# A hybrid transformer layer on one core: one weight tile loaded earlier, four pieces of work moved, and a second pool for the score banks

## The chip, the cores and the metric

The kernel runs on one core of a Trainium2 chip. The metric is the device time of one execution in microseconds. A comparison uses the median of several executions of each kernel on the same chip. A profile is one more execution, recorded by the hardware profiler; its span and its own time are given beside the medians.

## The reference

One layer (`DEPTH` is 1) of a backbone over 1024 latent tokens and 256 context tokens, `D_MODEL` 1024, all in float32:

```python
mod_x = (silu(c) @ w_ada + b_ada)           # six vectors: shift, scale, gate, twice
px = modulate(rms_norm(x, norm1_w), sh1, sc1) @ w_in     # latent tokens
pc = modulate(rms_norm(ctx, norm1_w), csh1, csc1) @ w_in # context tokens
# columns of w_in: q, k, v, z, a, b of a gated DeltaNet (4 heads of 128),
#                  q, k, v of a neighbourhood attention (8 heads of 64)
x = x + g1 * (concat([dn_x, na_x]) @ w_out)
x = x + g2 * swiglu(modulate(rms_norm(x, norm2_w), sh2, sc2), w_ffn_in, w_ffn_out)
```

The DeltaNet group passes q, k and v through a depthwise convolution of five taps and SiLU, normalises q and k, and runs a chunked scan in both directions, context first. For each chunk a unit triangular matrix has to be inverted. The attention group uses one softmax over a 16-wide window of eight rows and all context keys. Only the latent stream is returned.

## The kernel before, in words

Every large product is made with float32 operands that are split into a high part of type float32r (`hi`, `hh`, `whi`) and a rest (`lo`, `hl`, `wlo`), and takes three matmuls: high times high, high times rest, rest times high. The 1280 tokens lie along the free dimension in three segments of 256, 512 and 512 columns (`SEGS`), the model dimension in eight tiles of 128 partitions (`KT`).

*The start* (lines 665 to 778). SP loads the eight token tiles `xt` (640 KB each, line 680), two weight tiles `raws` (line 684) and the eight tiles `wada` of the first modulation weights (1024 KB each, `load_ada`, line 674). ACT squares the token tiles, DVE adds them in pairs (line 740), TensorE sums over partitions with a matrix of ones (line 742, two passes for each segment), and ACT turns the sums into the norm's factors `rs` (logarithm, line 744; exponential, line 745). `ada(j)` (line 701) multiplies one `wada` tile by the two conditioning vectors, 16 matmuls, and copies the row out; `column(j)` (line 710) turns that row into per-partition columns, four matmuls and two small DVE operations. `normed_tile(k)` (line 721) then makes `hh[k]` and `hl[k]` of token tile `k`: DVE multiplies (726), ACT adds the shift and rounds (727), DVE takes the rest (729). The first two key heads (`first`) are multiplied with each tile as it comes (lines 754 to 775). In this part the order of TensorE, DVE and ACT is written out by hand (`manual_schedule`): each of these engines runs its instructions in the order of the program text.

*The rest of the first half* (lines 1067 to 1157). The list `jobs` holds blocks of the input projection: key heads 0 to 3, one half of the gate z with the columns a and b (`Wide("z", 1)`), attention keys, values, queries and so on, in the end the other half of z (`Wide("z", 0)`). Each `Block` job has eight k steps (`mm([k])`); its `evac` copies the result to a tile `cacc`, of which there are two, and for q, k and v applies the five taps on DVE. As long as only the first PSUM pool exists (jobs 0 to 4), all banks come from one ring of eight, and DVE reads the taps straight from the block's three banks (line 455). `silu`, `norm` and the generator `finish` (line 530) follow one and two jobs later: for a key head `finish` makes three groups of transposes (line 537), three groups of products of the keys with themselves (line 561), and then a mask and stores. In a Block job one step of `finish` is taken after each k step from k = 3 on (line 1136), in a Wide job after each tile of tokens (line 1114), and what is left at the end of the job.

Outside the part written by hand, a planner puts the instructions on the engines: the order of the program text is their rank, and by its cost model it lets a later instruction go first where an earlier one is not ready; `keep_in_program_order` excepts single instructions from that. An engine then runs its list strictly in order, and waits where the model was wrong.

Two background lists are stepped along with the k steps. `bg` holds the block inverses and `preps` (line 948), which prepares the chunks for the scan: first products at L1000 from factors `rg` that POOL makes (line 988), an exponential, DVE's multiplication of `kk` (1011), products L1024, and three further levels (1035). Its first preparation is held back by `LATE` steps. `bg2` holds `modulation` (line 208), which makes the remaining modulation vectors: DVE accumulates weight rows (line 238), and `reduce` sums the result over partitions on TensorE (line 223), four steps after the last row where there is one accumulator.

[...] From job 5 on a pool `psa` gives four banks to blocks, two to `m`, two to `pr`. Ahead of the last job, `Wide("z", 0)`, it is closed and a pool `psg` opened, which holds two plain banks (`ps`) and two score tiles of three banks each (`sc`) of the attention; attention (`pair`, line 292) and scan then share TensorE until 790 us. The output projection and the feed-forward part follow with their own pool.

## Time and profile before

| | us |
|---|---|
| median of three runs | 1515.09 (1510.95 to 1518.55) |
| the profiled execution's own time | 1512.36 |
| its span | 1510.6 |
| TensorE busy | 1462.2 |
| VectorE (DVE) busy | 996.8 |
| ScalarE (ACT) busy | 703.5 |
| GpSimd (POOL) busy | 236.7 |

All times within the profile count from the start of its span. PE is TensorE, PEld its weight loads, SP the queue that issues most transfers. A line such as `PE m L223 <- DVE acc L238: 2.0, 1, 2.0` says that TensorE's instruction of line 223, which writes a tile `m`, waited for DVE's of line 238, 2.0 us in all, once, 2.0 us at most. A row of the time line gives start, duration, engine, line, operation, what it writes and reads, and in brackets how long the engine had been idle and who released it. A row of the stretches gives the stretch, its length, the busy time (with the count of instructions), the granted clock as a share of full speed, the share of the DMA engines that was busy, and GB/s.

### The profile page before, as it was taken

The page shows a single profiled execution, that of the slowest core. Times are in us where ns is not written, and L with a number is a line of the kernel's source. Part 1 is how long each engine was busy: PE and PEld are TensorE (multiplying, and loading weights), DVE is VectorE, ACT ScalarE, POOL GpSimd, SP SyncE. Part 2 cuts the span into 40 slices and gives each one's busy share as a digit, 9 for nine tenths or more (in the row PEclk, how much of TensorE's full clock was granted, in tenths as well). Part 3 has the DMA queues.
Part 4 walks back from the last instruction along what each step waited for, and adds up shares of the span by engine and source line. Part 5 has one row for each costly group of instructions (what it writes and reads, how often), then busy time and mean ns, then how long its engine had stood idle before and what let it go on. Part 6 is the DMA issues. An engine that isn't in the chain of part 4 may idle for free.

```text
span 1510.6 us, 23890 instructions
## 1 busy us (share of the span) xinstructions
PE 1462.2 (97%) x8702; PEld 1223.5 (81%) x8702; DVE 996.8 (66%) x1716; ACT 703.5 (47%) x1389; POOL 236.7 (16%) x286
## 2 busy tenths in 40 slices
PE   6999999999999998999999999999999999999998
PEld 3788797877788877887878888888888888888887
DVE  5773589875463745778867389766665567598652
ACT  5453442456663246656853284333333334354440
POOL 1054601456652201111210000000000000000000
PEclk9999999999999999999999999999999999999999
DMA  9274122778665569998539205433333335798742
GB/s 389 75 215 143 54 78 72 244 222 248 195 191 174 157 187 291 290 263 279 163 112 343 79 28 166 141 105 105 105 105 105 105 105 174 260 360 279 251 140 84
DMA packets 205398, 267.36 MB, mean 177 GB/s; under 512 B 15968, under 2 KB 113760, under 8 KB 204256
## 3 DMA queue, kind: packets, MB, share of 16 engines
q1 hardware_dynamic: 197680, 260.01, 53.2%
q10 hardware_dynamic: 7600, 5.81, 1.2%
q8 instruction: 69, 1.13, 0.3%
q14 instruction: 49, 0.40, 0.1%
HBM read 201.02 MB, written 68.94 MB: 179 GB/s over the span
## 4 chain that ended last, share of the span: by engine, by line
PE 51%; ACT 1%; DVE 1%; issue 0%; DMA 0%; POOL 0%; DVEq 0%; POOLq 0%; ACTq 0%
PE ps L1398 28%; PE ps L1741 14%; PE ps L1527 3%; PE ps L1375 1%; PE ps L1549 1%; PE sc L332 1%; PE sc L322 1%; PE sc L309 1%; PE ps L1252 0%; PE ps L1261 0%; DMA z<-z_d 0%; ACT sq L1302 0%; ACT bt L315 0%; DVE bt L313 0%; PE ps L223 0%
## 5 line engine op out<-in xcount | busy, mean ns | idle before, releaser
L1459 ACT CAST uhi<-wq 128x512 fp32r<-128x512 f32 x101 | 61.3, 622 | 135.9 <-issue 84.6
L413 PE MATMUL blk<-hh,whi 128*128 128x512 f32 (+1 forms) x410 | 121.0, 389 | 1.6 <-ACT kk L562 1.4
L1459 ACT CAST uhi<-ws 128x512 fp32r<-128x512 f32 x91 | 54.0, 621 | 146.3 <-PE ps L1398 91.4
L413 PE MATMUL blk<-hl,whi 128*128 128x512 f32 (+1 forms) x410 | 113.4, 370 | 0.3 <-DVE hl L729 0.3
L609 PE MATMUL blk<-zw,hh 128*128 128x256 f32 (+1 forms) x576 | 112.3, 289 | 1.0 <-ACT cr L461 1.0
L413 PE MATMUL blk<-hh,wlo 128*128 128x512 f32 (+1 forms) x410 | 112.0, 370 | 0.6 <-POOL wlo L204 0.6
L1460 DVE TENSOR_TENSOR ulo<-wq,uhi 128x512 fp32r<-128x512 f32 x101 | 67.6, 688 | 59.1 <-ACT uhi L1459 32.7
L1398 PE MATMUL ps<-hT,uhi 128*128 128x512 f32 x336 | 103.7, 390 | 0.0
L1398 PE MATMUL ps<-lT,uhi 128*128 128x512 f32 x336 | 103.4, 389 | 0.0
L1398 PE MATMUL ps<-hT,ulo 128*128 128x512 f32 x336 | 103.4, 389 | 0.0
L609 PEld LDWEIGHTS blk<-zw,hh 128*128 128x128 f32 x576 | 90.7, 189 | 4.1 <-ACT cr L461 1.4
L1398 PE MATMUL ps<-hB,uhi 128*128 128x512 f32 x288 | 89.1, 390 | 0.0
L1398 PE MATMUL ps<-lB,uhi 128*128 128x512 f32 x288 | 88.7, 389 | 0.0
L1398 PE MATMUL ps<-hB,ulo 128*128 128x512 f32 x288 | 88.7, 389 | 0.0
L413 PEld LDWEIGHTS blk<-hh,wlo 128*128 128x128 f32 x410 | 71.0, 188 | 14.8 <-POOL wlo L204 0.9
L413 PEld LDWEIGHTS blk<-hl,whi 128*128 128x128 f32 x410 | 71.2, 188 | 14.4 <-DVE hl L729 0.8
L609 PE MATMUL blk<-zw,hl 128*128 128x256 f32 (+1 forms) x288 | 81.9, 284 | 0.0
L413 PEld LDWEIGHTS blk<-hh,whi 128*128 128x128 f32 x410 | 67.6, 190 | 16.8 <-issue 3.8
L204 POOL TENSOR_TENSOR wlo<-wraw,whi 128x1024 fp32r<-128x1024 f32 x18 | 44.8, 2488 | 186.8 <-ACT whi L203 186.5
L1398 PEld LDWEIGHTS ps<-lT,uhi 128*128 128x128 f32 x336 | 63.1, 188 | 13.1
L1398 PEld LDWEIGHTS ps<-hT,ulo 128*128 128x128 f32 x336 | 63.1, 188 | 13.1
L1398 PEld LDWEIGHTS ps<-hT,uhi 128*128 128x128 f32 x336 | 62.9, 188 | 13.0
(361 smaller groups left out, 3500.7 us busy)
## 6 DMA issues: line engine op xcount, KB each, us to landing
wq<-w_fo SPq DMA_DIRECT2D x99, 256.0 KB, 4.2
wq<-w_gu SPq DMA_DIRECT2D x88, 256.0 KB, 2.9
wad<-wa SPq DMA_DIRECT2D x64, 256.0 KB, 4.3
bt<-rpb SPq DMA_DIRECT2D x64, 192.0 KB, 3.9
t_d<-g SPq DMA_DIRECT2D x22, 512.0 KB, 3.5
fr<-t_d SPq DMA_DIRECT2D x44, 256.0 KB, 4.9
f_d<-g SPq DMA_DIRECT2D x33, 256.0 KB, 2.1
fr<-f_d SPq DMA_DIRECT2D x33, 256.0 KB, 4.2
```

Source lines behind the costliest of these rows:

```text
L204: lo_engine.tensor_tensor(o, r, h.bitcast(F32), OP.subtract)
L309: s = pe.matmul(sc[:, u * 640 + n0:u * 640 + n1], q, ks[i], start=i == 0, stop=i == 1)
L322: pe.transpose(sc[:, u * 640 + j * 128:u * 640 + (j + 1) * 128], bt[:, j * 128:(j + 1) * 128], ident)
L332: pe.matmul(sc[u * ND:u * ND + ND, 1280:1408], vv, pt[:, j * 128:(j + 1) * 128], start=j == 0, stop=j == 4)
L413: pe.matmul(o, ww[:, k], xx[k][:, s], start=k == 0 and j == 0, stop=k == KT - 1 and j == 2)
L609: pe.matmul(p[:, :c1 - c0], x[k][:, s], ww[:, k, c0:c1], start=k == 0 and j == 0, stop=k == KT - 1 and j == 2)
L1375: pe.matmul(o, w[wi][:, k], parts[xi][k][:, s], start=k == 4 and j == 0, stop=k == 3 and j == 2)
L1398: pe.matmul(o, w[wi][:, k], x[xi][:, k], start=first and k == 0 and j == 0, stop=k == n - 1 and j == 2, skip_group_check=True)
L1459: act.copy(hi, self.raw[key])
L1460: dve.tensor_tensor(lo, self.raw[key], hi.bitcast(F32), OP.subtract)
L1527: pe.matmul(o, w[wi][:, k], parts[xi][k][:, s], start=k == 0 and j == 0, stop=k == KT - 1 and j == 2)
L1741: pe.matmul(o[b], w[wi][:, b], F[xn, p][xi], start=n in (0, 1, 5) and p == 0 and j == 0, stop=p == NFB // 2 - 1 and j == 2, skip_group_che ...
```

## The change

- `load_ada(0)` is issued between token tiles 3 and 4, and `ada(0)` and `column(0)` stand ahead of the third pair of squares.
- `normed_tile` is cut into `high` and `low`; the logarithm and exponential of each segment follow each other, and the first tile's `high` of a segment comes one segment later. The split of the first weights (`prefetch`) stands ahead of the logarithms. `ada(1)` stands behind the first six products, `column(1)` behind the second six.
- In job 3, `finish` of key head 1 starts at k = 5, not 3, and what is left at its end goes to the next job, one step after each tile, ahead of key head 2's.
- `reduce` of `modulation` with one accumulator comes six steps after the last row, not four.
- `LATE` is 6, not 7, and the first preparation has three steps, not two, between L1000 and L1024.
- Ahead of the last job a pool `psc` with the score tiles is opened first, and one score tile is taken at once; `psg` keeps the plain banks.

```diff
@@ -241,7 +241,7 @@
                     reduce(q - 1, prev)
             prev = acc2
             if sums == 1:
-                for _ in range(4):
+                for _ in range(6):
                     yield
                 reduce(q, prev)
                 prev = None
@@ -292,7 +292,7 @@
         def pair(heads, bts, vw, vc, half, cb, out):
             r0 = 4 * half
-            sc = psum[-1].tile([128, 1536], F32, name="sc", tag="sc", bufs=2)
+            sc = psc.pop() if len(psc) > 1 else psc[0].tile([128, 1536], F32, name="sc", tag="sc", bufs=2)
             mx = nw.tile([128, 2, 4], F32, name="mx", tag="mx", bufs=3)
             for u, (head, w0, bt) in enumerate(zip(heads, WIN, bts)):
                 qs, kh, kl = head
@@ -368,7 +368,7 @@
         next(old)
         store(*done)
-    na, kept = [], []
+    na, kept, psc = [], [], []
     def store(out, hp, half):
@@ -676,13 +676,15 @@
                 sp.dma_start(w, a["wa1"][j])
             for k in range(KT):
+                if k == 4:
+                    load_ada(0)
                 x = xp.tile([128, T], F32, name=f"xt{k}", tag=f"xt{k}")
                 sp.dma_start(x, a["xcT"][k])
                 xt.append(x)
             raws = [xp.tile([128, KT, 128], F32, name=f"fraw{i}", tag=f"fraw{i}") for i in range(2)]
             for i in range(2):
                 sp.dma_start(raws[i], a["w_conv"][4 + i])
-            for j in range(3):
+            for j in range(1, 3):
                 load_ada(j)
             sp.dma_start(cst, a["cst"])
             sp.dma_start(masks, a["masks"])
@@ -718,21 +720,28 @@
                                       [128, 2, 2]), OP.add)
                 dve.tensor_scalar(w1s[:, j], m[:, 1], 1.0, n1w[:, j:j + 1], op0=OP.add, op1=OP.mult)
-            def normed_tile(k, cuts=(slice(0, CT), slice(CT, T))):
-                t = xt[k]
-                parts = [(x, mod1[:, k, int(x.start < CT):int(x.start < CT) + 1]) for x in cuts]
-                for x, sh in parts:
-                    j = int(x.start < CT)
-                    dve.scalar_tensor_tensor(t[:, x], t[:, x], w1s[:, k, j:j + 1], rs[:, x], op0=OP.mult, op1=OP.mult)
-                    act.activation(hh[k][:, x], t[:, x], AF.Identity, bias=sh)
-                for x, sh in parts:
-                    dve.scalar_tensor_tensor(hl[k][:, x], t[:, x], sh, hh[k][:, x].bitcast(F32),
-                                             op0=OP.add, op1=OP.subtract)
+            def high(k, x):
+                t, j = xt[k], int(x.start < CT)
+                dve.scalar_tensor_tensor(t[:, x], t[:, x], w1s[:, k, j:j + 1], rs[:, x], op0=OP.mult, op1=OP.mult)
+                act.activation(hh[k][:, x], t[:, x], AF.Identity, bias=mod1[:, k, j:j + 1])
+
+            def low(k, x):
+                j = int(x.start < CT)
+                dve.scalar_tensor_tensor(hl[k][:, x], xt[k][:, x], mod1[:, k, j:j + 1], hh[k][:, x].bitcast(F32),
+                                         op0=OP.add, op1=OP.subtract)
+
+            def normed_tile(k):
+                for part in (high, low):
+                    for x in (slice(0, CT), slice(CT, T)):
+                        part(k, x)
             with tc.manual_schedule(engines={mybir.EngineType.PE, mybir.EngineType.DVE, mybir.EngineType.Activation}):
                 sums = [bank() for _ in SEGS]
                 segs = [slice(s0, s0 + n) for s0, n in SEGS]
                 for k in range(0, KT, 2):
+                    if k == 4:
+                        ada(0, dve.tensor_copy)
+                        column(0)
                     sq = [xp.tile([128, T], F32, name="sq%d" % i, tag="sq%d" % i, bufs=2 + i) for i in range(2)]
                     act.activation(sq[0], xt[k], AF.Square)
                     for s in segs if k == KT - 2 else [slice(0, T)]:
@@ -740,24 +749,28 @@
                         dve.tensor_tensor(sq[1][:, s], sq[0][:, s], sq[1][:, s], OP.add)
                     for p, s in zip(sums, segs):
                         pe.matmul(p[:, :s.stop - s.start], M[C_ONE], sq[1][:, s], start=k == 0, stop=k == KT - 2)
-                for p, s in zip(sums, segs):
-                    act.activation(rs[:, s], p[:, :s.stop - s.start], AF.Ln, bias=b_eps, scale=1.0 / D)
-                act.activation(rs, rs, AF.Exp, scale=-0.5)
                 first[0].prefetch(raws[0], dve, dve)
                 first[1].prefetch(raws[1], pool, pool)
-                ada(0, dve.tensor_copy)
-                column(0)
-                normed_tile(0, segs)
-                ada(1, act.copy)
+                for i, (p, s) in enumerate(zip(sums, segs)):
+                    act.activation(rs[:, s], p[:, :s.stop - s.start], AF.Ln, bias=b_eps, scale=1.0 / D)
+                    act.activation(rs[:, s], rs[:, s], AF.Exp, scale=-0.5)
+                    if i:
+                        high(0, segs[i - 1])
+                high(0, segs[2])
+                for s in segs:
+                    low(0, s)
                 for b in first:
                     b.banks()
                 for j, (w, x) in enumerate(((0, hh), (1, hh), (0, hl))):
-                    for b in first:
-                        for o, s in b.outs:
+                    for i in range(len(segs)):
+                        for b in first:
+                            o, s = b.outs[i]
                             pe.matmul(o, b.w[w][:, 0], x[0][:, s], start=j == 0, stop=False)
-                        if j == 0 and b is first[1]:
-                            column(1)
-                            normed_tile(1)
+                    if j == 0:
+                        ada(1, act.copy)
+                    if j == 1:
+                        column(1)
+                        normed_tile(1)
                 ada(2, act.copy)
                 column(2)
                 for k in range(1, KT):
@@ -1015,8 +1028,8 @@
                         if at is not None:
                             dve.tensor_tensor(at, at, e, OP.mult)
                             stores.append((at_d[d, c - 2], at, tick[0] + 2))
-                    yield 1
-                    yield 1
+                    for _ in range(2 if i else 3):
+                        yield 1
                     ps = []
                     for d, c, kk, xc, at in got:
                         p = bank("pr")
@@ -1040,7 +1053,7 @@
                     for d, c, kk, xc, at in got:
                         stores.append((y_d[d, c], y[d], tick[0] + 1))
-                LATE, stores, tick = 7, [], [0]
+                LATE, stores, tick = 6, [], [0]
                 def flush(n):
                     while stores and stores[0][2] <= n:
@@ -1078,7 +1091,7 @@
         def blk(n):
             return jobs[n] if 0 <= n < len(jobs) and isinstance(jobs[n], Block) else None
-        bg2, tail = Background(), None
+        bg2, tail, more = Background(), None, None
         bg2.add(modulation(adp, range(4), bank, 3, 1))
         first[0].evac()
         jobs[2].prefetch()
@@ -1102,6 +1115,9 @@
                 next(fill)
             if final:
                 psa.close()
+                psc.append(scan_psum.enter_context(tc.tile_pool(name="psc", bufs=1, space=PSUM)))
+                held_sc = psc[0].tile([128, 1536], F32, name="sc", tag="sc", bufs=2)
+                psc.append(held_sc)
                 psum.append(scan_psum.enter_context(tc.tile_pool(name="psg", bufs=1, space=PSUM)))
             if n + 1 < len(jobs):
                 jobs[n + 1].prefetch()
@@ -1110,7 +1126,10 @@
             nrm = blk(n - 1)
             if isinstance(j, Wide):
                 for t, _ in enumerate(j.tiles()):
-                    if t > 1 or not final:
+                    if more and next(more, 0) == 0:
+                        more = None
+                        done.add(n - 3)
+                    elif t > 1 or not final:
                         next(fin, 0)
                     if final and t > 4:
                         for _ in fin:
@@ -1133,15 +1152,18 @@
                         tail[0].norm()
                         tail[1].silu()
                         tail = None
-                    if k >= 3 and next(fin, 0) == 0:
+                    if k >= (5 if n == 3 else 3) and next(fin, 0) == 0:
                         done.add(n - 2)
                     bg.step(1)
                     if n > inv + 4:
                         bg2.step(1)
                 j.evac()
-            for _ in fin:
-                pass
-            done.add(n - 2)
+            if n == 3:
+                more = fin
+            else:
+                for _ in fin:
+                    pass
+                done.add(n - 2)
             if isinstance(j, Wide) and n == values:
                 vlat = nv_d[CT:].rearrange("(n r c) d -> r c n d", r=4, c=64)
                 for cb in range(4):
```

## The prediction

> **What bounds the kernel now.** The first view is the page's busy times, the second TensorE's busy time in six stretches of the span (microseconds, PE busy with its count, granted clock, DMA share, GB/s).
>
> ```profile
> PE 1462.2 (97%) x8702; PEld 1223.5 (81%) x8702; DVE 996.8 (66%) x1716; ACT 703.5 (47%) x1389; POOL 236.7 (16%) x286
> ```
>
> ```profile
> 0.00:52.00 52.00, 39.43 (x252) 0.93 0.79 311
> 52.00:130.00 78.00, 75.41 (x486) 1.00 0.53 160
> 130.00:300.00 170.00, 161.81 (x937) 0.99 0.36 109
> 300.00:540.00 240.00, 234.90 (x1727) 1.00 0.63 192
> 540.00:780.00 240.00, 224.27 (x2095) 1.00 0.79 240
> 780.00:1510.60 730.60, 726.40 (x3217) 1.00 0.47 159
> ```
>
> TensorE sets the time: it is busy for 1462.2 of 1510.6 us. The change leaves TensorE's work as it is and only reorders it, so all it can win is idle time and slow clock. Idle are 52.00 - 39.43 = 12.6 us in the first stretch, then 2.6, 8.2, 5.1, 15.7 and 4.2. The last 730 us, half of the run, are not touched by the diff. The third view names the idle time, by who waited for whom (total, times, longest):
>
> ```profile
> PE m L742 <- DVE sq L740: 10.6, 1, 10.6
> PE m L223 <- DVE acc L238: 2.0, 1, 2.0
> PE m L537 <- DVE cacc L455: 1.7, 1, 1.7
> PE pr L1024 <- DVE kk L1011: 1.2, 2, 0.8
> PE blk L609 <- ACT cr L461: 1.0, 1, 1.0
> ```
>
> Four of these five lines are where the diff edits something: 2.0 + 1.7 + 1.2 + 1.0 = 5.9 us, 0.4% of the run. The first is the wait for the first tokens; it stays.
>
> **The start.** A hand-written order holds here for TensorE, DVE and ACT, so the chain can be worked through. First the time line of before (start, duration, engine, line, idle before), then the DMA of one weight tile and three rows of stretches with clock and GB/s.
>
> ```profile
> 11.96 1.27 ACT L737 ACTIVATE sq<-xt 128x1280 f32<-128x1280 f32 x1 [0.35 <-DMA xt<-xcT]
> 14.79 1.49 DVE L740 TENSOR_TENSOR sq<-sq,sq 128x1280 f32<-128x1280 f32 x1 [1.65 <-ACT sq L739]
> 15.74 0.19 PEld L742 LDWEIGHTS m<-sq,ones 128*128 128x128 f32 x1 [0.24 <-issue]
> 19.38 0.47 ACT L744 ACTIVATE rs<-m,bias 128x256 f32<-128x256 f32 x1 [1.19 <-PE m L742]
> 19.64 1.94 DVE L204 TENSOR_TENSOR wlo<-fraw,whi 128x1024 fp32r<-128x1024 f32 x1
> 21.09 0.69 ACT L744 ACTIVATE rs<-m,bias 128x512 f32<-128x512 f32 x1 [0.17 <-PE m L742]
> 21.81 1.27 ACT L745 ACTIVATE rs<-rs 128x1280 f32<-128x1280 f32 x1
> 21.81 1.07 PE L706 MATMUL pm<-wada,wide 128*32 128x256 f32 x16 [0.76 <-DMA wada<-wa]
> 24.59 1.81 DVE L726 SCALAR_TENSOR_TENSOR xt<-xt,w1s,rs 128x256 f32<-128x256 f32 x3
> 28.87 0.85 PE L714 MATMUL pm<-bias,arow 128*128 128x2 f32 x4
> 31.43 1.34 PE L757 MATMUL blk<-hl,whi 128*128 128x256 f32 x6
> 31.93 1.15 ACT L727 ACTIVATE hh<-xt,mod 128x1024 fp32r<-128x1024 f32 x1 [0.69 <-DVE xt L726]
> 34.26 0.61 PE L714 MATMUL pm<-bias,arow 128*128 128x2 f32 x4 [0.49 <-ACT arow L708]
> 34.73 0.83 PE L413 MATMUL blk<-hh,whi 128*128 128x256 f32 x3
> ```
>
> ```profile
> wada<-wa SPq DMA_DIRECT2D x8, 1024.0 KB, 15.0
> ```
>
> ```profile
> 12.00:14.00 2.00, 2.00 (x3) 1.00 1.03 425
> 26.00:28.00 2.00, 2.00 (x8) 0.50 1.09 439
> ```
>
> ```profile
> 35.00:52.00 17.00, 17.00 (x150) 1.00 0.45 155
> ```
>
> *Won:* the norm's factors `rs` are ready at 21.81 + 1.27 = 23.08, but DVE's first use of them starts at 24.59, held by the modulation's weights (TensorE waited 0.76 for their DMA) and the column that is made of them. With `ada(0)` ahead this 1.5 us can go: the low end of my range for the start is -1.5.
>
> *Paid:* the 1024 KB of weights now go ahead of token tiles 4 to 7. At 425 GB/s they take 1.05 MB / 425 = 2.5 us, so the square that waited for its tile until 11.96 starts near 14.4, and the pair that DVE added at 14.79 is ready for it near 17.3. TensorE ends the sums of the second pair about 15.74 + 2 x 0.43 = 16.6 (a pass is 0.24 + 0.19 in the row) and only then takes `ada(0)`. From the start of `ada(0)` to DVE's next work were 24.59 - 21.81 = 2.8 us; so DVE, which keeps its order, adds the third pair at 19.4, not at 17.3, and ends at 20.9. TensorE, free for that pair at 16.6 before, starts it at 20.9: the sums are 4.3 us later, and the logarithms stand at 23.7 to 25.4 instead of 19.38 to 21.09. DVE's adds, cast and split of the first weights (some 2.5, estimated, and 1.94) end near 25.4 and its first `high` at 25.9; on ACT follow that `hh` (about 0.5), the last logarithm (0.69), its exponential (about 0.65, estimated from 1.27 for 1280 columns) and two `hh` of some 0.7, a half of 1.15 and its start: 29.2. The last of the first six products ends near 29.7. From the second weight tile on, the order and the bytes ahead are as before, and POOL's split of the other weights, 2.5 us later, is needed only at 30.8: no cost.
>
> Then, in the new order, `ada(1)` 1.07, six products with `wlo` (1.34, the row of `hl`), and `column(1)` at 32.1. Before, `column(1)` began at 28.87 and the second tile's `hh` ended at 31.93 + 1.15 = 33.08, 4.2 us behind; a quarter of a microsecond of that was slow clock (0.85 there, 0.61 for the same at 34.26). So that `hh` ends near 36.1, the copy for `column(2)` comes behind it on ACT, and the second tile's products, at 34.73 before, start about 37.0. **Start: +2.3 us at full clock.** TensorE idles for some 2 us between `column(0)` and the third pair, and again between the sums and the first `hh`. Before had a slow spell too (0.50 at 26 to 28); I charge 0.7 for longer ones: **+3.0**. The high end is 4.3 more (two pairs of sums, each five times 0.43, at half clock): +6.6. From 35 to 52 TensorE is busy without a gap, so what is late there stays late.
>
> [...]
>
> **The key transposes** (job 3, key head 1).
>
> ```profile
> 97.49 1.04 ACT L203 CAST whi<-wraw 128x1024 fp32r<-128x1024 f32 x1 [4.55 <-DMA wraw<-w_nqk]
> 108.67 1.63 ACT L446 ACTIVATE cacc<-blk,cw 128x256 f32<-128x256 f32 x3
> 115.05 0.44 PE L537 MATMUL m<-cst,cacc 128*128 128x128 f32 x2
> 117.77 1.27 ACT L476 ACTIVATE cacc<-cacc 128x1280 f32<-128x1280 f32 x1 [4.92 <-DVE cacc L455]
> 126.64 0.60 PE L537 MATMUL m<-cst,cacc 128*128 128x128 f32 x4
> ```
>
> ACT stood 4.55 us for a weight's DMA, so the first transposes were not copied out and the third had no bank until DVE let one go: the 1.7 us. Two k steps later ACT is past that cast: -1.7. But head 1's products of keys with keys now follow the third tile of the gate, where head 2's transposes stood at 115.05, and they hold head 1's `cacc`, one of two. Head 3's evacuation, at 108.67 before, needs it: about 115.7, 7.0 us later, and its SiLU ends near 126.0, not 119.04. Its transposes stood at 126.64: 0.6 us of slack are left. Unknown cost, between 0 and 7.0 less 0.6; I take 0.5, nearest to the row with its slack: **-1.2**. The stores of heads 1 and 2 also leave later on SP; their readers, the preparations, come after 290.
>
> **Column sums and first preparation.**
>
> ```profile
> 292.99 1.14 PE L223 MATMUL m<-ones,acc 128*128 128x1 f32 x8 [2.01 <-DVE acc L238]
> 294.00:295.00 1.00, 1.00 (x4) 0.50 1.13 308
> 294.70 1.48 POOL L988 TENSOR_TENSOR rg<-GL,cst 128x512 fp32r<-128x512 f32 x1
> 297.12 0.42 PE L1000 MATMUL pr<-rg,mr 128*128 128x512 f32 x1
> ```
>
> Two steps later the sum `acc` is there: -2.0 (the next columns wait two steps for its buffer, on DVE, which TensorE needs only at their own sums); and the clock, 0.50 after this gap, stays up: between 294.13 and 297.12 that is 1.5 us. But TensorE then reaches the first preparation (297.12) 3.5 us earlier, at 293.6, while POOL's last factor ends at 294.70 + 1.48 = 296.18. Three matmuls ahead of it take some 1.4 us, so about 1.2 us of wait come back: **-2.3** (between -3.5, and +1 if `LATE` = 6 brings TensorE a step ahead of POOL). The products L1024 wait 1.2 us in all for DVE; one step more covers it: **-1.2** (0 to -1.2). Later preparations keep their distances; their waits are dealt anew, ±1.5.
>
> **Other score banks.** The gate's last block waits 1.0 us at L609 for ACT to empty the three `blk` banks of the values. With the score pool opened first, its plain tiles lie in the last two banks, which nothing then reads: **-1.0** (0 if the wait holds for the whole old pool).
>
> **Sum.** +3.0 - 1.2 - 2.3 - 1.2 - 1.0 = -2.7 us, on the profiled execution's own 1512.36 (span 1510.6 and 1.8 around it): 1509.7. The median of the three runs, 1515.09, is 2.7 above that execution; for a median to come I take the middle, **1511**.
>
> **Rivals.**
> - *The start costs nothing* (-1.5 in place of +3.0: the sums run warm earlier, and DVE's split fits between). Sum -7.2: 1505. For it: 1.5 us of DVE idle before 24.59. Against: the 2.5 us of DMA and the 2.8 us of `ada(0)` stand ahead of the sums.
> - *Slow sums*: +6.6 at the start, sum +0.9: 1513.3. For it: 0.50 at 294 after 2.01 us of idle. Against: in before only two such spells.
> - *The third `cacc`* ends on the other side: if DVE puts more than 0.6 us of other work (modulation rows, reductions) between head 3's twelve taps, TensorE waits at head 3's transposes for up to 6.4 us, and the gain of 1.2 becomes a loss of 4.7: sum +3.2, 1515.6; with slow sums 1519. Against: those transposes may be passed by the gate's tiles.
> - *The banks don't do what they say*: 1510.7, within the forecast.
>
> **Chances.** What a measurement of this kernel tells from no change is about 0.5%, 7.6 us. Forecast (1506 to 1514 on the profiled base) 0.50; start free 0.22; slow sums 0.13; third `cacc` 0.15. Faster by over 0.5% (under 1504.8) is the lower half of the second and a tail of the first: 0.17. Slower is the joint end of the last two: 0.08. Within: 0.75. The range reaches from 1504, the free start less the spread of later waits, to 1518, the third `cacc` on the median.
>
> **What would show it.** Right: the second tile's products (L413) start after 36 us; no wait at L223, at L609 for `cr`, at L1024; a wait or none at L1000 below 1.5 us; head 3's evacuation L446 near 115 us; the clock at 294 is 1.00. Wrong: the sums end before 23 us, or a new wait over 3 us stands anywhere between 120 and 140 us or in the scan stage, whose order a planner sets anew.

## The result and the profile after

The changed kernel takes 1523.4 us (median of 8 runs, 1520.76 to 1526.08), before 1515.67 (8 runs, 1510.95 to 1518.55): ratio 1.0056, 95% interval 1.0041 to 1.0071. The change makes the kernel slower; 1511, in a range of 1504 to 1518, was forecast. The profiled execution took 1521.93 us, span 1520.0. First its busy times, then two of the six stretches (microseconds, busy time with counts of PE, PEld, DVE, ACT and POOL, granted clock, DMA share, GB/s).

```profile
PE 1466.7 (96%) x8702; PEld 1224.6 (81%) x8702; DVE 993.6 (65%) x1716; ACT 703.9 (46%) x1391; POOL 237.1 (16%) x286
```

```profile
0.00:52.00 52.00, 34.99 (x193) 20.32 (x194) 25.37 (x40) 24.82 (x33) 5.32 (x8) 0.90 0.78 306
...
300.00:540.00 240.00, 234.73 (x1683) 196.34 (x1684) 135.93 (x173) 123.33 (x240) 112.10 (x133) 0.98 0.65 199
```

The work is the same 8702 matmuls, but TensorE is busy 4.5 us longer (1466.7 against 1462.2), so some of them ran at a lower clock (0.98 from 300 to 540 us, 1.00 before); and 4.4 us less of them lie in the first 52 us (34.99 against 39.43). The span grew by 9.4 us. The checkpoint for the start is ACT's evacuation of the first head, one row of before and one of after:

```profile
66.46 0.47 ACT L446 ACTIVATE cacc<-blk,cw 128x256 f32<-128x256 f32 x1
```

```profile
72.77 0.47 ACT L446 ACTIVATE cacc<-blk,cw 128x256 f32<-128x256 f32 x1
```

That is +6.3 us. The same comparison of evacuations further on gives +6.5 at 244 us, +7.5 at 340, +8.9 at 493, +9.4 at the end. So two thirds of the loss are made before the first head, and nothing is won back later. The start in the time line of after (line numbers are each kernel's own from here on):

```profile
14.83 1.27 ACT L746 ACTIVATE sq<-xt 128x1280 f32<-128x1280 f32 x1 [2.86 <-DMA xt<-xcT]
18.01 0.61 PE L716 MATMUL pm<-bias,arow 128*128 128x2 f32 x4 [0.55 <-DVE arow L710]
18.99 3.02 DVE L749 TENSOR_TENSOR sq<-sq,sq 128x1280 f32<-128x1280 f32 x4
20.52 6.06 PE L751 MATMUL m<-sq,ones 128*128 128x256 f32 x12 [1.91 <-DVE sq L749]
24.91 0.47 ACT L755 ACTIVATE rs<-m,bias 128x256 f32<-128x256 f32 x1 [3.87 <-PE m L751]
27.11 0.51 ACT L726 ACTIVATE hh<-xt,mod 128x256 fp32r<-128x256 f32 x1
29.68 0.72 ACT L726 ACTIVATE hh<-xt,mod 128x512 fp32r<-128x512 f32 x1 [0.21 <-DVE xt L725]
31.60 1.94 PE L708 MATMUL pm<-wada,wide 128*32 128x256 f32 x16
34.88 0.50 PE L716 MATMUL pm<-bias,arow 128*128 128x2 f32 x4
39.05 0.61 PE L716 MATMUL pm<-bias,arow 128*128 128x2 f32 x4 [1.42 <-ACT arow L710]
39.52 0.83 PE L413 MATMUL blk<-hh,whi 128*128 128x256 f32 x3
```

The chain is the one that was forecast: tile 4's square at 14.83 (forecast 14.4), DVE held by the column until 18.99 (19.4), then all later than forecast: first logarithm 24.91 (23.7), last `hh` ended at 30.40 (29.2), second column 34.88 (32.1), second tile's products 39.52 (37.0). TensorE's clock in three stretches of 2 us:

```profile
21.00:23.00 2.00, 2.00 (x4) 1.04 (x4) 1.97 (x4) 0.04 (x1) 0.89 (x1) 0.50 1.01 418
31.00:33.00 2.00, 2.00 (x18) 0.59 (x16) 0.36 (x1) 0.00 (x0) 0.00 (x0) 0.50 1.03 426
41.00:43.00 2.00, 2.00 (x16) 0.89 (x18) 1.51 (x2) 1.31 (x2) 0.00 (x0) 0.50 0.34 88
```

Three spells of half clock, 3.41 us each (20.2 to 23.6, 30.4 to 33.8, 40.7 to 44.1): they meet the sums, `ada(1)` with the next products, and the second tile. Before had 6.83 us of it in its start. Over the first 800 us there are 20.5 us at half clock, in before 10.2. Then TensorE's waits in after:

```profile
PE blk L768 <- ACT hh L726: 2.6, 3, 1.3
...
PE pr L1013 <- POOL rg L1001: 2.4, 4, 0.9
...
PE pr L1048 <- POOL y L1027: 1.9, 1, 1.9
...
PE m L537 <- ACT cacc L476: 1.4, 1, 1.4
...
PE blk L609 <- ACT cr L461: 1.0, 1, 1.0
```

Of the four waits that the edits aim at, those at L223 (2.0), L537 for DVE (1.7) and L1024 (1.2) are gone. In their place stand 2.4 at L1013 (L1000 before) and 1.9 at L1048 (L1035 before), both for POOL, and 1.4 at L537 for ACT: 5.7 us for 4.9. The wait of 1.0 at L609 for `cr` stands as it was.

### The profile page after: what moved, and what is told of

It reads as the page before. It is cut to its first block, busy times and chain, and to the rows that moved or that the text cites. A ratio compares the mean times of both kernels' runs of the same rounds, so it can differ in the third digit from the quotient of the medians.

```text
span 1520.0 us, 23891 instructions
## 1 busy us (share of the span) xinstructions
PE 1466.7 (96%) x8702; PEld 1224.6 (81%) x8702; DVE 993.6 (65%) x1716; ACT 703.9 (46%) x1391; POOL 237.1 (16%) x286
## 4 chain that ended last, share of the span: by engine, by line
PE 51%; ACT 1%; DVE 0%; issue 0%; DVEq 0%; ACTq 0%
PE ps L1420 28%; PE ps L1763 14%; PE ps L1549 3%; PE ps L1397 1%; PE ps L1571 1%; PE sc L332 1%; PE sc L309 1%; PE sc L322 1%; PE ps L1295 0%; PE ps L1274 0%; PE ps L1283 0%; ACT sq L1324 0%; DVE bt L313 0%; PE ps L223 0%; ACT pt L325 0%; PE ps L1300 0%
## 5 line engine op out<-in xcount | busy, mean ns | idle before, releaser
L609 PE MATMUL blk<-zw,hh 128*128 128x256 f32 (+1 forms) x576 | 112.8, 291 | 1.0 <-ACT cr L461 1.0
L1482 DVE TENSOR_TENSOR ulo<-wq,uhi 128x512 fp32r<-128x512 f32 x101 | 67.7, 689 | 59.3 <-ACT uhi L1481 32.8
L609 PEld LDWEIGHTS blk<-zw,hh 128*128 128x128 f32 x576 | 91.3, 190 | 4.3 <-ACT cr L461 1.4
L609 PE MATMUL blk<-zw,hl 128*128 128x256 f32 (+1 forms) x288 | 82.1, 285 | 0.0
L413 PEld LDWEIGHTS blk<-hh,whi 128*128 128x128 f32 x410 | 67.7, 190 | 17.3 <-issue 4.2
```

Of the source, the lines that this page charges most:

```text
L413: pe.matmul(o, ww[:, k], xx[k][:, s], start=k == 0 and j == 0, stop=k == KT - 1 and j == 2)
L609: pe.matmul(p[:, :c1 - c0], x[k][:, s], ww[:, k, c0:c1], start=k == 0 and j == 0, stop=k == KT - 1 and j == 2)
L1482: dve.tensor_tensor(lo, self.raw[key], hi.bitcast(F32), OP.subtract)
```

## Experiments

Two theories were tested first. *Order*: the start is late because bytes and DVE's work are put ahead of the sums. *Clock*: the new idle gaps set TensorE to half clock, and the order alone would cost little. The ratios are against runs of before on the same chip; "first head" is the start of the L446 row above.

| run | median us | ratio, 95% interval | first head |
|---|---|---|---|
| e1 new start alone | 1521.57 | 1.0047, 1.0031 to 1.0063 | 72.22 |
| e2 all but the start | 1517.32 | 1.0013, 0.9999 to 1.0026 | |
| e3 column sums alone | 1518.79 | 1.0021, 1.0008 to 1.0033 | |
| e4 key transposes alone | 1516.26 | 1.0002, 0.9988 to 1.0016 | |
| e5 start, 31 fillers | 1520.61 | 1.0040, 1.0027 to 1.0053 | 71.71 |
| e6 weights' DMA alone | 1517.33 | 1.0011, 0.9999 to 1.0022 | 68.38 |
| e7 order behind the sums | 1519.66 | 1.0025, 1.0015 to 1.0036 | 70.74 |
| e8 start, column later | 1522.79 | 1.0049, 1.0031 to 1.0067 | 73.61 |
| e9 start, `ada(1)` earlier | 1518.80 | 1.0014, 1.0003 to 1.0026 | 70.79 |
| e10 start, old tail | 1520.30 | 1.0031, 1.0018 to 1.0044 | 70.64 |
| e11 banks by tile | 1515.72 | 0.9991, 0.9977 to 1.0005 | |
| e12 first preparation alone | 1516.04 | 0.9997, 0.9984 to 1.0011 | |
| e13 start, 6 fillers | 1522.36 | 1.0050, 1.0034 to 1.0065 | 73.22 |
| e14 before with fillers | 1520.07 | 1.0032, 1.0019 to 1.0045 | |
| e15 column sums, fillers | 1516.59 | 1.0010, 0.9998 to 1.0023 | |
| e16 e13, second weights later | 1518.93 | 1.0034, 1.0021 to 1.0047 | 71.92 |
| e17 e9, second weights later | 1520.67 | 1.0050, 1.0030 to 1.0070 | 70.86 |
| e18 before, loads and banks | 1515.35 | 1.0013, 1.0002 to 1.0023 | |

**e1 and e2: which half.** e1 is before with the hunks of the diff from `load_ada(0)` to `normed_tile(1)`; e2 is the change without them.

> The kernel before with the new start alone (first weight tile amid the tokens, ada(0) and column(0) ahead of the third pair, the new order behind the sums). Theory 1, the loss is made at the start and stays: the evacuation of the first key head (L446) comes 6.3 us later than in before, as in after, and the median is 5.5 to 7 us above before. Rival, the start's delay is taken up later by waits that become shorter: the first evacuation is late by 6.3 us, the median by 3 us or less.

> The change without its start (sums, preparation, key transposes and score banks only). Theory 1: 0 to +3 us on before, since in after the stretch behind 66 us lost 3.1 us more. Rival, the other edits gain 5.9 us once the late start no longer meets them: 4 to 6 us below before.

The start alone costs 0.47%, 7.1 us, the rest 0.13%, 2 us: together 0.60%, the change 0.56%. So the start makes the loss, and the rest brings nothing that can be told from no change.

**e6 and e7: the start's two parts.** e6 moves only the DMA, e7 only the order behind the sums.

```diff
+                if k == 4:
+                    load_ada(0)
...
-            for j in range(3):
+            for j in range(1, 3):
                 load_ada(j)
```

```diff
-                ada(1, act.copy)
...
-                        if j == 0 and b is first[1]:
-                            column(1)
-                            normed_tile(1)
+                    if j == 0:
+                        ada(1, act.copy)
+                    if j == 1:
+                        column(1)
+                        normed_tile(1)
```

> Only the DMA of the first modulation weights goes amid the tokens; the order of the instructions is that of before. Theory (the 1024 KB hold back token tiles 4 to 7 by 2.5 us and the sums with them): the square of the fifth tile starts near 14.4 instead of 11.96, the first logarithm near 21.9 instead of 19.38, and DVE's first use of the norm's factors at 26.4 to 27.1 instead of 24.59; L446 of the first head 1.8 to 2.5 us later where the clock is the same; the run 1516.5 to 1517.5. Rival (the weights' own wait of 0.76 us and the 1.5 us for the column were the bound, so what the tokens lose is won there): first use within 0.7 of 24.59, the run within 1 of before.

> Only the order behind the sums is changed (exponentials by segment, highs ahead of lows, the six first products by segment, second copy of modulation behind the first six products, second column behind the next six); DMA and first column stay where they were. Theory (the move of the second column and tile behind twelve products costs by itself): the second tile's products L413 start 1.5 to 2.5 us later than 34.73 and the run takes 1516 to 1517.5. Rival (only the move of the weights and of the first column ahead of the sums costs): L413 within 0.5 of 34.73 at the same clock and the run within 1 of before.

The time line of e6: first logarithm, first use by DVE, second tile.

```profile
21.96 0.47 ACT L746 ACTIVATE rs<-m,bias 128x256 f32<-128x256 f32 x1 [1.04 <-PE m L744]
26.65 1.81 DVE L728 SCALAR_TENSOR_TENSOR xt<-xt,w1s,rs 128x256 f32<-128x256 f32 x3
36.65 0.84 PE L413 MATMUL blk<-hh,whi 128*128 128x256 f32 x3
```

The bytes put the logarithm 2.6 us later (19.38 before), the second tile 1.9 (34.73), the first head 1.9. The ratio, 1.7 us, cannot be told from no change, but each row agrees with the theory. The time line of e7: second segment's `hh`, second column, second tile.

```profile
27.05 0.71 ACT L724 ACTIVATE hh<-xt,mod 128x512 fp32r<-128x512 f32 x1
32.85 0.50 PE L714 MATMUL pm<-bias,arow 128*128 128x2 f32 x4
37.49 0.87 PE L413 MATMUL blk<-hh,whi 128*128 128x256 f32 x3
```

The second tile is 2.8 us late, beyond the 1.5 to 2.5 expected: the second `hh` comes 1.3 later than before (25.77), since on ACT the third segment's logarithm and exponential (0.67 and 0.63) now stand behind the first `hh`, which waits for the column; the second column comes 4.0 later. The run costs 0.25%, 3.8 us, and its median is above the expected 1516 to 1517.5. So the order loses by itself, and by the rows the bytes do too.

**e8, e9, e10: pieces put back.** e8 takes `column(0)` behind the sums; e9 takes `ada(1)` ahead of the first products and `column(1)` behind the first six; e10 is e9 with the old logarithms and one exponential.

```diff
                     if k == 4:
                         ada(0, dve.tensor_copy)
-                        column(0)
...
+                column(0)
                 first[0].prefetch(raws[0], dve, dve)
```

```diff
+                ada(1, act.copy)
                 for b in first:
                     b.banks()
...
                     if j == 0:
-                        ada(1, act.copy)
-                    if j == 1:
                         column(1)
```

> The new start, but the first column goes behind the sums; its modulation stays ahead of them. Theory (DVE, held by the column ahead of the third pair, makes the sums late): the third pair's add starts 1.2 us earlier than the 18.99 of the change, near 17.8, the sums end 1.2 us earlier, and L446 of the first head comes near 71.5; the run 1520. Rival clock (the spells decide, not the microsecond): L446 is earlier by a multiple of about 1.7 or not at all, by how many spells of 3.41 us fall into 18 to 52 us.

> The new start, but the second copy of modulation stands ahead of the first six products, where TensorE waits anyway, and the second column with the second tile behind those six instead of behind twelve. Theory late column (the later place of the second column costs 1.07 for its weights' products and 1.34 for six products on the path): the second tile's products L413, at 39.52 in the change, come near 37.3 (36.9 to 37.9), and the run takes near 1519.5. Rival (what is late is the first tile itself, its logarithms and its DMA, and the column follows it): L413 within 0.7 of 39.3 and the run near 1521.5.

> Weights and first column amid the tokens, but behind the sums the old order: all logarithms, one exponential, the second modulation ahead of the first products, the second column behind the first six. Theory late column and logarithms: beside the run with the second modulation moved back, the logarithm of the third segment no longer stands behind the first hh on ACT, which saves another 0.5 to 1.3 us: L413 near 36.6 to 37.2, the run 1517.5 to 1518.5, within 1 of the run with the weights' DMA alone (1517.3, L413 36.65): having the column early is then worth nothing. Rival (the exponentials by segment save time, as they were meant to): L413 later than in the run with the second modulation moved back.

e8 missed both of its expectations. In this execution `ada(0)` starts at 18.01, in after at 16.39, so the third pair's add starts at 19.49 and not near 17.8; less that 1.6 us the theory holds so far, and the first logarithm comes at 23.91 (24.91 in after). But DVE then has the column ahead of its cast and split, and its first use comes at 28.16 (25.86 in after).

e9 is 2.8 us below e1 by the medians and 5.0 by the ratios; the late column is thus part of the loss, though its second tile, 39.05, missed the range: half clock lies from 30.5 to 37.3.

In e10 the first `hh` starts 4.3 us behind the first logarithm (25.71, 29.97), in e9 2.2 (24.97, 27.16): the exponentials by segment do save time, as the rival had it, though its second tile, 38.91, is not the later one; e9's start has 3.41 us more at half clock.

Against e6, e10 has the column ahead (and the six products by segment): DVE starts the third pair's add at 19.60 and not at 17.53, and the first head is 2.3 us later, with 3.41 us more at half clock. The ratios differ by 0.20%, and their intervals overlap: **the early column gains nothing, and by the rows it costs.**

**e5 and e13: the clock alone.** `fill_pe(n)` issues n products of ones into a bank that nothing reads; e5 has 31 in four gaps, e13 only the six behind `column(0)`.

```diff
                         ada(0, dve.tensor_copy)
                         column(0)
+                        fill_pe(6)
```

> The new start alone, with 31 small products of ones added on TensorE in its idle gaps (8 behind the first column, 12 behind the sums, 5 in the first products, 6 ahead of the third column); they write a bank that nothing reads, so the work grows and the output does not change. Theory clock (a good half of the start's loss is TensorE at half clock behind the new idle gaps): no spell of 0.50 between 18 and 52 us, or one instead of three; each of 3.41 us costs 1.7, so the first head's evacuation L446, at 72.77 in the change and 66.46 before, comes at 67.7 to 69.4, and the run takes 1517 to 1519. Rival order (the loss is the order of DMA and DVE, and the clock only falls into time that is idle anyway): L446 stays within 0.7 of 72.5 and the run stays near 1521.5, the time of the start alone.

> The new start alone, with six small products of ones (some 1.5 us) in the one gap between the first column and the sums of the third pair; they write a bank that nothing reads. Theory clock (the gap of 1.91 us sets the sums to half clock): no spell of 0.50 between 20 and 26 us; the sums of the last two pairs, 20.52 to about 26.5 in the change, take 1.5 less, and the first head's evacuation L446 comes 1.5 to 3 us earlier than the 72.22 of the start alone, 69.2 to 70.7; the run 1518.5 to 1520. Rival order: L446 within 0.7 of 72.2, the run near 1521.5, whatever the clock shows.

In e5 no spell is left between 18 and 52 us, and the first head still comes at 71.71, 5.3 after before, nearer to the rival than to the theory. Its rows show two causes that neither of them had (DVE's adds, POOL's split, TensorE's last sums):

```profile
20.52 6.01 DVE L756 TENSOR_TENSOR sq<-sq,sq 128x1280 f32<-128x1280 f32 x4
22.98 2.40 POOL L204 TENSOR_TENSOR wlo<-fraw,whi 128x1024 fp32r<-128x1024 f32 x1
25.98 1.98 PE L758 MATMUL m<-sq,ones 128*128 128x512 f32 x4 [1.08 <-DVE sq L756]
```

DVE's four adds ahead of the sums take 6.01 us, in after 3.02. One of them, on 512 columns, took 2.83 us and not 0.68 as in after; it ended at 25.93, 0.55 after POOL's split (22.98 + 2.40 = 25.38). From the first logarithm to the end of the last `hh` e5 takes 7.2 us, after 5.5. And `ada(0)` starts at 17.92, in after at 16.39: the first sums ran at half speed until 16.5 us, there until 13.7 (0.85 us from one product of 512 columns to the next, then 0.43; the clock rows show 1.00 for both). Without these 1.7 and 1.5 us the first head would come at 68.5, an estimate that lies in the range of the theory (67.7 to 69.4). So e5 does not decide between the two.

In e13 the spell of the sums is gone; time line:

```profile
20.83 4.56 PE L758 MATMUL m<-sq,ones 128*128 128x256 f32 x12 [0.47 <-DVE sq L756]
22.23 1.53 DVE L201 CAST whi<-fraw 128x1024 fp32r<-128x1024 f32 x1
23.71 0.47 ACT L762 ACTIVATE rs<-m,bias 128x256 f32<-128x256 f32 x1 [3.06 <-PE m L758]
23.79 3.26 DVE L204 TENSOR_TENSOR wlo<-fraw,whi 128x1024 fp32r<-128x1024 f32 x1
26.97 1.13 DVE L725 SCALAR_TENSOR_TENSOR xt<-xt,w1s,rs 128x256 f32<-128x256 f32 x2
```

```profile
21.70 1.50 POOL L201 CAST whi<-fraw 128x1024 fp32r<-128x1024 f32 x1 [16.16 <-DMA fraw<-w_conv]
23.29 2.68 POOL L204 TENSOR_TENSOR wlo<-fraw,whi 128x1024 fp32r<-128x1024 f32 x1
```

The sums take 4.56 instead of 6.06, the logarithm comes 1.2 us earlier than in after, and nothing is won: DVE's cast and split took 1.53 and 3.26 instead of 0.69 and 1.94, the first use slips from 25.86 to 26.97, and ACT waits 1.56 us for it. Then half clock follows from 27.6 to 34.4 and from 41.3 to 44.7, 10.2 us in all, as much as in after. So to take away the first spell gained nothing by itself: another engine was late, and the next gap was followed by the next spell. What the start would take without half clock and without POOL in DVE's way, no run shows.

**e16 and e17: DVE against POOL.** The split of DVE ends at 27.05, 1.08 after POOL's split (23.29 + 2.68 = 25.97); the cast ends 0.56 after POOL's cast. So in both pairs DVE's instruction, longer than in after, ended only behind POOL's. e16 is e13, e17 is e9, with POOL's weights loaded 2.5 us later.

```diff
-            for i in range(2):
-                sp.dma_start(raws[i], a["w_conv"][4 + i])
-            for j in range(1, 3):
+            sp.dma_start(raws[0], a["w_conv"][4])
+            load_ada(1)
+            sp.dma_start(raws[1], a["w_conv"][5])
+            for j in range(2, 3):
                 load_ada(j)
```

> The run with six fillers, with the DMA of the second first-pass weights behind that of the second modulation tile, so that GpSimd's cast and split begin some 2.5 us later than VectorE's. Theory contention (the cast and split of VectorE are slow when GpSimd's ran first): VectorE's cast takes 0.69 and its split at most 1.94, the first use of the norm's factors starts near 24.9 instead of 26.97, the first head's evacuation L446 1.5 to 2.5 us before the 73.22 of the run with fillers, 70.7 to 71.7; the run 1520 to 1521. Rival (GpSimd is as late as it is slow, so its own weights now hold the first products): VectorE is fast, but a wait for whi or wlo of the second weights stands in front of the first products, and L446 stays at 73 or later.

> The new start with the second modulation moved back ahead of the first products, and the same later load of the second weights; no fillers. Theory contention: the first products' second six or TensorE's clock decide, VectorE's cast and split take 0.69 and at most 1.94 as in the run with the second modulation alone (where GpSimd happened to begin late), so this profile is the same within its clock: the run 1518 to 1519. Rival (that run's median hides executions with the slow split): the median falls to 1516.5 to 1517.5.

Time line of e16:

```profile
22.75 0.68 DVE L201 CAST whi<-fraw 128x1024 fp32r<-128x1024 f32 x1
23.47 1.22 DVE L204 TENSOR_TENSOR wlo<-fraw,whi 128x1024 fp32r<-128x1024 f32 x1
25.67 2.42 POOL L204 TENSOR_TENSOR wlo<-fraw,whi 128x1024 fp32r<-128x1024 f32 x1
26.47 2.17 DVE L726 SCALAR_TENSOR_TENSOR xt<-xt,w1s,rs 128x512 f32<-128x512 f32 x1 [0.60 <-ACT rs L764]
```

Ahead of POOL's, cast and split take 0.68 and 1.22, and the first use comes at 25.19, 1.8 earlier. The first head is 1.3 earlier, less than the 1.5 to 2.5 expected; it has 6.8 us of half clock where e13 has 10.2, so not all of that need be contention. And the collision only moved: DVE's second `high` now meets POOL's split, takes 2.17 us (the third, on as many columns, 0.75 in after) and ends at 28.64, 0.55 after POOL's 28.09. So the rows show the contention, while its price in the whole run is not shown (1.0034 against 1.0050, with intervals that overlap). e17 is slower than e9 (1.0050 against 1.0014), with its first head where it was (70.86 and 70.79); neither of its expectations held (1518 to 1519, and 1516.5 to 1517.5), and why it is slower stays open.

**e3, e15, e12: column sums and first preparation.** e3 is one number; e15 adds fillers ahead of the products that then wait for POOL (their results are overwritten); e12 is the step and `LATE` of the first preparation.

```diff
-                for _ in range(4):
+                for _ in range(6):
                     yield
                 reduce(q, prev)
```

```diff
                         p = bank("pr")
+                        for _ in range(3 if i == 0 else 0):
+                            pe.matmul(p[:, :128], ones, ones, start=True, stop=True)
...
+                        for _ in range(4 if i == 0 and n == 1 else 0):
+                            pe.matmul(ps[0][:, 0], ones, ones, start=True, stop=True)
```

```diff
-                    yield 1
-                    yield 1
+                    for _ in range(2 if i else 3):
+                        yield 1
...
-                LATE, stores, tick = 7, [], [0]
+                LATE, stores, tick = 6, [], [0]
```

> Before with the column sums two steps later alone (reduce after six steps, not four). Theory: the 2.0 us of wait at L223 and the slow clock behind it go, and 1 to 2.5 us come back as waits of L1000 for POOL's factors: 1 to 2.5 us below before. Rival, everything comes back because POOL sets the time of the first preparation: within 0.7 us of before, with 2 to 3.5 us of waits at L1000.

> Kernel before with the column sums two steps later, as in the third run, and with fillers ahead of the products that then wait for GpSimd (three ahead of each pair of L1000 in the first preparation, four ahead of its first L1035); the fillers' results are overwritten. Theory clock (the 3 us that the later sums cost are mostly spells of half clock behind those waits): no spell between 290 and 312 us where that run had three windows of 3.41; the run back at 1515 to 1516.5. Rival waits (GpSimd's rate, 1.45 us for each of four factors, is the bound, and TensorE's clock in between is worth nothing): L1000's waits for rg and the filler in front of them still add up to 2.5 to 3 us and the run stays near 1518.8.

> Kernel before with one more step between the factors and the products of the first preparation, and LATE at 6. Theory (the wait at the products L1024 for DVE, 1.2 us in all before, goes; the planner's other steps stay): no wait at L1024, the checkpoints of ACT at 318 to 522 us 1.2 earlier where no new spell of 0.50 falls, the run 1514. Rival (each wait that is removed ahead of POOL's and DVE's chains comes back one step later, as with the column sums): the waits of the stretch 290 to 320 us have the same sum, at L1000 or L1035 instead, and the run is within 1 of before.

Time line of e3, the first and last of four such rows and the next wait; then its clock in two stretches, and the same two in e15.

```profile
289.76 0.50 PE L1000 MATMUL pr<-rg,mr 128*128 128x512 f32 x1 [0.42 <-POOL rg L988]
...
294.10 0.69 PE L1000 MATMUL pr<-rg,mr 128*128 128x512 f32 x1 [0.71 <-POOL rg L988]
305.58 0.63 PE L1035 MATMUL pr<-y,kk 128*32 128x32 f32 x8 [1.13 <-POOL y L1014]
```

```profile
304.00:308.00 4.00, 2.87 (x14) 2.02 (x14) 1.84 (x3) 1.65 (x3) 3.58 (x10) 0.56 0.81 237
308.00:312.00 4.00, 4.00 (x25) 2.81 (x24) 0.35 (x1) 1.54 (x3) 3.42 (x5) 0.59 0.03 10
```

```profile
304.00:308.00 4.00, 4.00 (x36) 3.23 (x36) 2.48 (x5) 0.81 (x2) 3.63 (x9) 1.00 0.27 70
308.00:312.00 4.00, 4.00 (x29) 3.64 (x28) 0.00 (x1) 3.95 (x6) 4.00 (x3) 1.00 0.04 13
```

TensorE now meets POOL's four factors one by one, 1.45 us apart (289.76 to 294.10 in three steps), waits 2.8 us for them and 1.1 for POOL's copies, and stands at half clock for 6.8 us behind that. Between the evacuations at 244 and 340 us the stage takes 3.6 us longer than before in e3 and 0.2 in e15. The fillers, which do nothing but keep TensorE busy, leave one spell of 3.41 us in this stage (at 291.5), where e3 has 13.6 us of half clock. But 1.1 of e3's 3.6 us fall ahead of 275 us, behind a spell at 260, and e4, e11 and e12, which lack this edit, have such a one as well. And e2, which has this edit and waits as long (2.8 and 1.5), but 3.41 us of half clock, takes 0.6 us less than before. So the profiles agree with the clock theory: the waits come back, and it is the spells behind them that make the loss. The ratios (1.0021 and 1.0010) do not tell e3 and e15 apart.

e12 leaves the wait at L1024 at 2.4 us, which e4, without that edit, has too (2.3), and with 1.1 at L223 and a new 0.9 for POOL at L1035 its waits in this stretch are no less than before's 3.2: the step is worth nothing, as the rival had it.

**e4: key transposes.** The hunks with `more` and `n == 3`.

```diff
-                    if k >= 3 and next(fin, 0) == 0:
+                    if k >= (5 if n == 3 else 3) and next(fin, 0) == 0:
```

> Before with the later key transposes alone. Theory, as read from after: the 1.7 us wait at L537 for cacc goes and 1.4 us come at another L537, for the SiLU of key head 2, whose transposes the planner pulls ahead; the median within 1 us of before, head 3's evacuation 7 to 8 us late and hidden. Rival, the 1.4 us belong to the late start and not to this edit: 1.7 us below before.

```profile
108.19 0.66 PE L537 MATMUL m<-cst,cacc 128*128 128x128 f32 x4 [1.39 <-ACT cacc L476]
```

The wait of 1.7 is gone and one of 1.4 is new: head 2's transposes, next in line, now reach TensorE before ACT has done head 2's SiLU. No gain.

**e11: the banks, made to do what they say.** The edit of the banks, with both pools opened so:

```diff
-                psum.append(scan_psum.enter_context(tc.tile_pool(name="psg", bufs=1, space=PSUM)))
+                psum.append(scan_psum.enter_context(tc.tile_pool(name="psg", bufs=1, space=PSUM, reuse_waits="tile")))
```

> Kernel before with the other score banks, and both new pools waiting for their tiles' own banks instead of for the whole pool that was closed. Theory (the edit of the banks gave nothing because the first tile of a new pool waits for all readers of the old one): the wait of TensorE at L609 for cr, 0.97 us before and after, is gone or under 0.2, and the run is 1 us shorter, 1514 (not to be told from no change). Rival (the wait is that of the tile's own banks, or of the data): 0.97 stays.

The waits of TensorE at L609 in e11:

```profile
PE blk L609 <- ACT kk L562: 1.1, 1, 1.1
...
PE blk L609 <- ACT zg L640: 0.5, 1, 0.5
```

The wait for `cr` is gone; one of 0.5 for `zg` is new. (That of 1.1 for `kk` stands in e15 too, which has the banks of before.) So the edit of the banks fails because the new pool waits for the whole closed one. Its 0.09% less is not to be told from no change.

**e14 and e18: can before be beaten?** e14 is e11 with two fillers in each of two gaps of the old start and five ahead of each single column sum; e18 is e11 with `load_ada(0)` ahead of the load of `raws[1]`.

```diff
             p = bank()
+            for _ in range(5 if sums == 1 else 0):
+                pe.matmul(p[:, 128:256], ones, ones, start=True, stop=True)
```

```diff
+            sp.dma_start(raws[0], a["w_conv"][4])
+            load_ada(0)
+            sp.dma_start(raws[1], a["w_conv"][5])
```

> Kernel before with the score pools waiting by tile (worth the 0.97 us at L609) and fillers: two small products in each of two gaps of the old start and five ahead of the single column sums. Theory (gaps of 0.8 to 2 us ahead of busy stretches cost a spell of 1.7 us each, and the fillers hold the clock): no spell at 24 to 31 us and at 294, the run 1.0 + 1.7 + 1.7 shorter than before: 1511 to 1513. [...]

> Kernel before with the score pools waiting by tile (0.97 us at L609) and the load of the first modulation weights ahead of the second first-pass weights. Theory (the first column comes earlier by the 0.76 us that TensorE waited for these weights, and VectorE's split, without GpSimd beside it, takes 1.22 instead of 1.94): first use of the norm's factors near 23.9 instead of 24.59, no wait at L609 for cr, together 1.7 us: the run 1512.5 to 1513.5. Rival (GpSimd, 2.5 us later, is late with the second weights): a wait for them in front of the first or the second six products, 1514 to 1516.

e14 has no spell in the start, as expected, and its first head comes at 65.76; but a spell that was to go at 294 stands at 296.5, and the run is 0.32% slower: the five fillers stand ahead of all four column sums, where one had a gap, and its preparations then wait for POOL as in e3 (0.95, 1.24 and 0.72 us). e18 is 0.13% slower, and its first use comes at 25.54, not near 23.9. TensorE took the modulation's weights earlier, and POOL's split met DVE again:

```profile
23.06 2.35 POOL L204 TENSOR_TENSOR wlo<-fraw,whi 128x1024 fp32r<-128x1024 f32 x1
23.98 1.46 DVE L720 TENSOR_SCALAR w1s<-mod,prm 128x2 f32<-128x2 f32 x1
```

An operation on 2 columns, 0.23 us elsewhere, ends with POOL's split, at 25.44 and 25.41. No version was found that beats before by more than can be told.

## Why the prediction was wrong

By stages of the profile, forecast and measured (evacuations at 66, 244 and 340 us, end): start +3.0 and +6.3; key transposes -1.2 and +0.2; column sums with the products L1024 -3.5 and +1.0; from there to the end -1.0 (the banks) and +1.9, a spell at 436 us in it. In all -2.7 and +9.4. Of the 12.1 us between them, 3.3 lie in the start and 8.8 in the credits; by the ratios of e1 and e2 (7.1 and 2 us) it is 4.1 and 7.7. So two steps failed. The start decides that the change loses, and the credits make the larger part of the miss.

**The first is the sum's first term, "Start: +3.0".** Its order of events was right: the 2.5 us of bytes (2.6 in e6), DVE held by the column, the second column behind twelve products, the second tile after 36 us. Its size was off: +6.3 in the profile, 7.1 by the ratio of e1. The prediction put +2.3 on the order at full clock and "0.7 for longer ones", the spells. After shows +4.8 at the second tile and 1.5 more at the first head, about the price of one spell of 3.41 us. What was mis-sized most, as far as the profiles show, is the clock. The old start without a spell has its first head at 64.5 to 64.7 (e2, e3, e15), and the profile of before, with 6.83 us of half clock, at 66.46. After's 72.77 less 1.7 for each of its three spells is 67.7. By this estimate (not all of a spell need lie on the path) the order costs some 3 us, where 2.3 were forecast, and the clock some 3 more than in before, where 0.7 were.

The rival "slow sums", +6.6 at the start with a chance of 0.13, came near by number, and that is luck: it put 4.3 us on the sums, which took 1.5 us longer (6.06, and 4.56 in e13), and the other two spells lie behind them. What it rests on was known, though: the gap of 1.91 us ahead of the third pair was seen beforehand ("some 2 us"), and so was half clock behind a gap of 2.01 us. The spells in these starts lasted 3.41 us, or two or three times that; in after the first set in at 20.2, inside the gap of 1.91 that ended at 20.52.

That step also called POOL's split "no cost". It can hold DVE, and the trace of before showed it already:

```profile
19.24 1.26 POOL L201 CAST whi<-fraw 128x1024 fp32r<-128x1024 f32 x1 [13.63 <-DMA fraw<-w_conv]
```

POOL's cast ends at 20.50, DVE's split at 21.58, 1.08 later; alone it takes 1.22 (e18), not 1.94. In the old order DVE's cast starts 0.3 us ahead of POOL's; with the column amid the tokens that lead was 0.2 in after and lost in e1, e10 and e13. In the profile of after itself this is not on the path: DVE's split ends at 24.59, and from the first logarithm (24.91) to the last `hh` ACT has one pause, of 0.21. In e1 it makes the last add of the sums 0.84 us longer, in e13 ACT waits 1.56 for it, and e5 is held most. How the 7.1 us of the median divide between order, clock and this stays open: the cure of one brought out the next (e5, e13, e16).

**The second is the credits, -5.7 in all, which came to nothing.** "Column sums: -2.3": the wait at L223 went, but "about 1.2 us of wait" became 2.4 at L1013 and 1.9 for POOL's copies. The step reckoned with POOL's last factor alone, as if TensorE had the other three by then; it gets one each 1.45 us. (`LATE` = 6, for which the prediction allowed up to +1, is not the reason: e3, where it is 7, has these waits too.) That the clock "stays up": it does at 294, and falls at 300 and 314, behind the new waits (in the first 800 us behind the start, after has three spells and before one). Alone the edit costs 0.21% (e3). "L1024: -1.2": the wait is absent in after, where POOL's copies hold TensorE instead, and the edit alone does not remove it (e12). "Key transposes: -1.2": between 66 and 244 us +0.2, as a wait that was not foreseen, for head 2's own SiLU, took the place of the old one (e4). What was foreseen, head 3's evacuation 7.0 us later, is there (108.67 to 122.79, less 6.3 is 7.8) and costs nothing. "Banks: -1.0": the bound "0 if the wait holds for the whole old pool" is what happened, shown by e11.

Right were the base, TensorE as the bound, and the bound given for the banks. The sign was wrong, and a loss of over 0.5% had been given a chance of 0.08.

## What to carry to other kernels

When an engine that is the bound meets its suppliers earlier, look at the rate of each supplier over the next ten microseconds, not at its last item: here the waits that the column sums and the key transposes removed came back at the next supplier. A gap of about 2 us was followed by half clock in five profiles of six ahead of the third pair, and in nine of twenty near 430 us: here it is to be priced with the half clock behind it (by estimate up to 1.7 us, half of each spell of 3.41) in the base case, not only in a tail. When work is moved on DVE, look at what POOL does in the same microsecond.

## What the runs showed of the hardware

Half clock came in spells of 3.41 us (six in the first 800 us of after), or two or three times that (6.83 in before's start, 10.24 in e11's), and whether a gap was followed by one differed from execution to execution. The gap of 1.9 us ahead of the third pair was followed by one in after, e1, e9, e10 and e17, not at once in e8; cut to 0.5 us by fillers, in neither profile (e13, e16). The same wait of 1.9 us for `y` near 430 us was followed by a spell in nine of the twenty profiles (after, e2, e3 and e15 among them) and by none in the others (before, e4, e11 and e18 among them). So the unchanged start puts the first head anywhere from 64.5 to 68.2 us (seven profiles: before, e2, e3, e4, e11, e12, e15; mean 66.4): at 64.5 to 64.7 in the three without half clock there, at 66.5 to 68.2 in the four with 6.83 or 10.24 us of it. Single profiles are to be compared by stage, with the clock beside them.

DVE and POOL delay each other in these rows. Six times a DVE instruction that met one of POOL ended 0.03 to 1.08 us after it (twice in e13, once in e5, e16, e18 and before), and took longer than elsewhere: DVE's split 1.94 us in before and 3.26 in e13, against 1.22 in e16 and e18; the operation on 2 columns 1.46 in e18, against 0.23. And POOL's cast, 1.04 us in e18, where DVE idles for most of it, took 1.26 in before and 1.40 in after, beside DVE's cast and split. It is not so for every pair: in before, DVE's copy of a row out of PSUM (22.94 to 23.37) ran in its usual 0.42 us inside POOL's split (20.58 to 23.80); and in e16 DVE's split, which began at 23.47, took no longer than in e18, though POOL's cast began at 24.12, inside it. What the two engines share, no run shows.
